# A two-layer hybrid attention block on one core: another order of loads, transposes and splits in the opening stage

## The chip, the cores and the metric

One core of a Trainium2 chip runs the whole program. The metric is device time in microseconds, the median of three runs; lower is better. Five engines work side by side: PE (TensorE: products and transposes), DVE (VectorE), ACT (ScalarE), POOL (GpSimd), and SP (SyncE), which here only issues DMAs. ACT and POOL issue DMAs too.

## What is computed

Two layers over 512 latent tokens `x` and 256 context tokens `ctx`, 1024 features each, all in fp32. Cut to what the change touches, which is the beginning of layer 0:

```python
c_act, c_ctx_act = silu(c), silu(c_ctx)                       # two vectors of 1024
sh1, sc1, g1, sh2, sc2, g2 = split(c_act @ w_mod[l] + b_mod[l], 6)      # the same from c_ctx_act for ctx
h_x = x * (1 + sc1) + sh1
h_c = ctx * (1 + csc1) + csh1
px, pc = h_x @ w_in[l], h_c @ w_in[l]                         # then three token mixers, merge, norm, FFN
```

`w_mod[l]` is 1024 by 6144. Of its twelve column blocks of 512, blocks 0 and 1 give the shift `sh1`, blocks 2 and 3 the scale `sc1`; only these four are needed before the first product with `h`. The other eight blocks of layer 0 are made later, between other work, and are not touched.

## The kernel before

Products are taken at fp32 precision by splitting: each operand is a `hi` part (rounded to fp32r by a cast) and a `lo` part (the rest, by a subtraction), and a product is three matmuls (`mm3`). So weights and activations are cast (usually on ACT) and subtracted (DVE, or POOL for some weights) before PE may use them. The activations `h` are kept feature-major: `h[0]` (hi) and `h[1]` (lo) are tiles of 128 by 8 by 768 fp32r.

All instructions are emitted inside `tc.manual_schedule()`: each engine runs its own instructions in the order in which the program emits them, and waits for what an instruction needs while later ones of that engine stand behind it. `Clock` (line 110) is a forecast kept by the program while it emits; `weave` (line 433), `At` and `Need` use it to decide how many steps of weight products are emitted between two steps of a latency-bound chain. `pump` (line 332) emits the loads of weights ahead into three `wr` buffers and one `wrf` buffer; `do_conv` (line 365) emits their splits.

The opening stage before the change:

- `setup` (line 501) makes silu of `c` and `c_ctx`; `setup_rows` (line 522) loads small parameters by POOL.
- `mod_block(0, blk, True)` (line 612) for blk 2, 0, 3, 1 makes four jobs each. A job loads 256 rows of `w_mod` (512 KB). Its products have 2 or 4 columns of `c` as the stationary side and 512 columns of weights moving. Of each block the first and last quarter are split (cast, subtract), the two in the middle go to PE as raw fp32. After the fourth quarter ACT copies the sums out of PSUM, and `post` (line 617) transposes them to columns.
- `build` (line 1789) emits the jobs of blocks 2 and 0 until the scale block 2 is done, then four loads of `x` on ACT's queue, then weaves `start0` (line 1807). That one issues three loads of the first 416 columns of `w_in` on ACT's queue, and then goes through `x` in two halves of the features: half 0 as soon as blocks 2 and 0 are there, half 1 after blocks 3 and 1. `mod_half` (line 780) transposes four blocks of a token tile to PSUM and applies scale and shift straight from PSUM (token tiles by turns on ACT and DVE); `mod_split` (line 797) of a tile is emitted after `mod_half` of the next one.
- The context tiles follow one by one (`mod_tile`, line 772), between the latent tiles' products with those 416 columns (`b1_tile`, line 821). The jobs of `win_jobs` (line 970), tiles of 128 other columns of `w_in`, fill PE in between; the first three are dq0, dk0 and dv0.
- `setup_cols` (line 543) and `setup_late` (line 561) are emitted after the last split of the latent tokens.

The line numbers of all calls in the profile are L106, the helper through which every instruction is emitted; so groups are told apart by their tiles: `wr`, `wh`, `wl` are a raw weight tile, its hi and lo part; `c` and `cact` the silu vectors; `ln` token tiles; `ac` and `h` scaled tokens and their split; `bc` the raw 416 columns and `s<-bc` their split; `b` and `S` are PSUM.

```python
self.split(hi, lo, src):   nc.scalar.copy(hi, src);  (lo_eng or nc.vector).tensor_tensor(lo, src, hi.bitcast(F32), ALU.subtract)
```

Of the kernel before, what the change touches and what calls it, by code (L numbers as in the profile page):

```python
# [97 lines left out]
class Port:  # L98
    """an engine's queue, each instruction noted by the clock before it is emitted"""
# [10 lines left out]
class Clock:  # L110
    """A coarse forecast, in us, of when each engine gets to what is put in its queue and when each tile is written.
    It only decides how many steps of the weight products are put between two steps of a latency-bound chain."""
# [63 lines left out]
    def transfer(self, t, c):  # L176
        """the first free stretch of the DMA rings from t on"""
# [44 lines left out]
class At:  # L222
    """go on when the products put in the queue reach this time"""
# [18 lines left out]
class Kern:  # L242
# [257 lines left out]
    # ---------------------------------------------------------------- setup  # L500
# [21 lines left out]
    def setup_rows(self):  # L522
        """loads of the small parameters, as rows"""
# [37 lines left out]
    def setup_late(self):  # L561
        nc, I, cp = self.nc, self.I, self.cp
        self.mask = cp.tile([P, NLEV, P], U8, name="mask")
        mv = self.mask[:].rearrange("p a b -> p (a b)")
        for a, b in ((0, 512), (512, NLEV * P)):
            mf = self.slab()
            nc.sync.dma_start(mf[:, :b - a], I["k_mask"][:, a:b])
            nc.vector.tensor_copy(mv[:, a:b], mf[:, :b - a])
        self.rm = cp.tile([P, TX], F32, name="rm")
        nc.sync.dma_start(self.rm[:], I["k_rope_m"])  # L570
        self.rk = cp.tile([P, 4, 2, 32], F32, name="rk")
        nc.sync.dma_start(self.rk[:].rearrange("p a b c -> p (a b c)"), I["k_rope_k"])
# [38 lines left out]
    # ---------------------------------------------------------------- adaLN modulation vectors  # L611
    def mod_block(self, l, blk, direct=False):
        nc, I = self.nc, self.I
        st = {}
        sec, half = blk // 2, blk % 2

        def post(mr):
# [19 lines left out]
            self.done.add(f"mod{l}_{blk}")  # L637

        def mk(u):
# [5 lines left out]
            def body(job):  # L645
# [5 lines left out]
                for k2 in range(2):  # L651
                    if job.conv is not None:
                        nc.tensor.matmul(ps[:2, :], self.cact[:].rearrange("p (a k) -> p k a", a=2)[:, 2 * u + k2, :],
                                         job.raw[:, k2 * 512:(k2 + 1) * 512], start=False, stop=False)
                        continue
# [3 lines left out]
                if job.conv is not None:  # L659
                    self.rawout[job.rk] -= 1  # L660
# [4 lines left out]
            j = Job(body, load, 1024)  # L665
            if direct:
                j.late = True
                if u in (1, 2):
                    j.conv, j.hold = (lambda j: None), True
            return j  # L670
# [86 lines left out]
    def affine(self, key, l, which, ln):  # L757
        """per-feature gain and offset of x -> x * (1 + sc) + sh, after the gain and offset of a layer norm if any"""
# [13 lines left out]
    def mod_tile(self, key, t, xo, h):  # L772
        """h[:, :, tile t] = transpose(xo) * A + B, split in two parts"""
# [35 lines left out]
    # ---------------------------------------------------------------- latent query/key front  # L809
# [185 lines left out]
    # ---------------------------------------------------------------- multi-head latent attention  # L995
# [136 lines left out]
    # ---------------------------------------------------------------- differential attention  # L1132
# [196 lines left out]
    # ---------------------------------------------------------------- bidirectional gated recurrence  # L1329
# [186 lines left out]
    # ---------------------------------------------------------------- gated merge  # L1516
# [132 lines left out]
    def ln_front(self, x1, r):  # L1649
        """x1 <- ALPHA * r + x1; the scale and offset of its normalization"""  # L1650
# [74 lines left out]
    # ---------------------------------------------------------------- FFN  # L1725
# [63 lines left out]
def build(ctx, tc, I, out):  # L1789
# [17 lines left out]
    def start0(xin):  # L1807
        K.b1w = []
        raws = [K.b1_load(0, u, K.nc.scalar.dma_start) for u in range(3)]
        prev = None  # L1810
        for g in range(2):
            for blk in ((2, 0), (3, 1))[g]:
                yield Need(f"mod0_{blk}")
            for i, t in enumerate(XT):
                hx = K.fp.tile([P, TX], F32, tag="ac", bufs=4, name=K.nm("ac"))
                yield from K.mod_half("in0", t, xin[t], g, hx[:], (K.nc.scalar, K.nc.vector)[i % 2])
                if prev:
                    yield from K.mod_split(K.h, *prev)
                prev = t, g, hx[:]
                if g == 1:  # L1820
                    yield At(K.ck.ready(raws[0]))
                    K.b1_conv(raws.pop(0))
                    if i == 0:
                        raws.append(K.b1_load(0, 3, K.nc.sync.dma_start))
            if g == 0:
                yield Need("mod0_3")
                for t in CT:
                    K.nc.scalar.dma_start(xin[t][:], res[t])
        yield from K.mod_split(K.h, *prev)
        K.done.add("hx0")  # L1830
        K.setup_cols()
# [15 lines left out]
    with tc.manual_schedule():  # L1847
# [3 lines left out]
        for blk in (2, 0, 3, 1):  # L1851
            for j in K.mod_block(0, blk, True):
# [141 lines left out]
```

## Time and profile before

| | |
|---|---|
| median of 3 runs | 3069.2 us (3064.12 to 3072.55) |
| span of the profiled execution | 3064.3 us |
| PE busy | 2825.8 us, 92% of the span |
| DVE, ACT, POOL busy | 53%, 37%, 32% |
| mean granted TensorE clock | 0.961 |
| moved by DMA | 359.14 MB, mean 117 GB/s |

The page gives the span of the profiled execution and no other time of it; the span is 4.9 us below the median of the runs and close to the fastest of them. "PEclk" is the granted share of TensorE's clock: 1.00 is 2.4 GHz and 0.50 is 1.2 GHz, and a value between is a stretch with both. A row of the timeline reads: start, duration, engine, line, operation, out<-in, shapes, count, and in brackets the idle time before it and what ended it. SPq, ACTq and POOLq are a queue's issues of DMAs; the duration of such a row is that of the issue, waits between merged issues included, not that of the transfer.

### The profile page before, as it was taken

Reading aid. Unit: us, or ns where it says so; the run is one execution under the profiler, and the core shown is the slowest. Engines: PE = TensorE matmul, PEld = TensorE weight load, DVE = VectorE, ACT = ScalarE, POOL = GpSimd, SP = SyncE. Lnnn points to the kernel's source line nnn. Section 1 sums busy time; section 2 is a strip of 40 time slices with the busy share of each in tenths; the row PEclk is TensorE's granted clock in tenths of the full one; section 3 lists DMA queues with packets and bytes.
Section 4 is the critical chain, followed back from the end, with each engine's and each line's share of the span. In section 5 each row is a group of like instructions: output and inputs, shape, how many; then the busy total and the mean of one; then the engine's idle time right before and its main releaser. Section 6 shows DMA issues by size and latency. Waiting matters only on the chain. (4 is left out here: it accounts for less than half of the span.)

```text
span 3064.3 us, 39087 instructions
## 1 busy us (share of the span) xinstructions
PE 2825.8 (92%) x14899; PEld 2346.2 (77%) x14899; DVE 1628.7 (53%) x2413; ACT 1137.7 (37%) x2177; POOL 974.2 (32%) x688
## 2 busy tenths in 40 slices
PE   6999989998799997999999898999998899799997
PEld 3888866677688885888888677887776777688875
DVE  4455566657762038555543665445656762632235
ACT  4544434443332124344332445444444332322222
POOL 1333433334444434243320223333324555300002
PEclk8999999999999998999999999999999999899998
DMA  6423243343333354354443354324223343433331
GB/s 211 129 80 97 91 136 96 100 141 103 101 111 110 103 169 151 117 152 143 119 137 96 110 167 122 89 83 131 79 73 127 104 132 123 146 107 96 103 131 69
DMA packets 345523, 359.14 MB, mean 117 GB/s; under 512 B 31114, under 2 KB 263044, under 8 KB 345336
## 3 DMA queue, kind: packets, MB, share of 16 engines
q1 hardware_dynamic: 343144, 351.84, 37.0%
q10 hardware_dynamic: 1680, 4.42, 0.4%
q8 instruction: 117, 1.92, 0.3%
q14 instruction: 70, 0.57, 0.1%
q0 software_dynamic: 512, 0.39, 0.1%
HBM read 298.10 MB, written 58.49 MB: 116 GB/s over the span
## 5 line engine op out<-in xcount | busy, mean ns | idle before, releaser
L106 PE MATMUL b<-h,wh 128*128 128x512 f32 (+1 forms) x5152 | 1385.0, 358 | 32.2 <-ACT h L106 14.2
L106 PEld LDWEIGHTS b<-h,wh 128*128 128x128 f32 x5152 | 911.5, 193 | 168.3 <-ACT h L106 15.1
L106 PE MATMUL b<-h,wl 128*128 128x512 f32 (+1 forms) x2576 | 909.5, 353 | 0.0
L106 DVE TENSOR_TENSOR wl<-wr,wh 128x1024 fp32r<-128x1024 f32 (+1 forms) x253 | 373.0, 1478 | 458.3 <-ACT wh L106 457.3
L106 PEld LDWEIGHTS b<-h,wl 128*128 128x128 f32 x2576 | 496.6, 193 | 66.4 <-DVE wl L106 0.3
L106 ACT CAST wh<-wr 128x1024 fp32r<-128x1024 f32 (+1 forms) x298 | 295.0, 993 | 415.2 <-PE b L106 331.2
L106 POOL TENSOR_TENSOR sm<-sm,mhalf 128x1 f32<-128x1 f32 (+3 forms) x80 | 56.7, 709 | 1035.7 <-DVE sm L106 1035.7
L106 POOL TENSOR_TENSOR wl<-wr,wh 128x1024 fp32r<-128x1024 f32 (+1 forms) x131 | 285.5, 2179 | 222.4 <-ACT wh L106 199.9
L106 ACT ACTIVATE s<-S,sm 128x768 f32<-128x768 f32 (+1 forms) x170 | 135.2, 796 | 377.7 <-DVE sm L106 325.2
L106 POOL TENSOR_TENSOR ln<-ln,wr 128x512 f32<-128x512 f32 x84 | 119.5, 1423 | 222.9 <-issue 161.6
L106 PE MATMUL S<-wh,ac 128*128 128x512 f32 x512 | 173.8, 404 | 16.4 <-DVE ac L106 11.2
L106 PE MATMUL S<-k,s 128*128 128x128 f32 (+2 forms) x704 | 150.8, 336 | 37.8 <-DVE k L106 33.8
L106 DVE TENSOR_TENSOR k<-b,k 128x512 fp32r<-128x512 f32 (+1 forms) x136 | 85.0, 627 | 175.0 <-ACT k L106 174.7
L106 PE MATMUL S<-k,k 96*128 96x512 f32 (+2 forms) x576 | 153.0, 366 | 22.8 <-DVE k L106 11.8
L106 PE MATMUL b<-k,wh 128*128 128x512 f32 (+1 forms) x576 | 161.5, 368 | 10.5 <-ACT k L106 6.9
L106 DVE TENSOR_REDUCE sm<-S 128x1 f32<-128x768 f32 (+1 forms) x160 | 131.5, 839 | 70.1 <-PE S L106 70.0
L106 PEld LDWEIGHTS S<-k,s 128*128 128x128 f32 (+1 forms) x704 | 107.4, 207 | 76.8 <-issue 51.2
L106 PEld LDWEIGHTS S<-k,k 96*128 96x128 f32 (+1 forms) x576 | 103.5, 196 | 63.4 <-issue 16.9
L106 PE MATMUL b<-ident,s 128*128 128x128 f32 (+3 forms) x687 | 111.8, 276 | 42.5 <-DVE s L106 19.3
L106 POOL TENSOR_SCALAR wh<-wr 128x1024 fp32r<-128x1024 f32 (+1 forms) x86 | 88.7, 1036 | 188.5 <-PE b L106 179.3
L106 POOL TENSOR_TENSOR s<-s,s 128x512 f32<-128x512 f32 (+2 forms) x88 | 112.4, 1288 | 90.2 <-DVE s L106 45.6
L106 DVE TENSOR_TENSOR k<-s,k 96x768 fp32r<-96x768 f32 (+7 forms) x92 | 108.8, 1209 | 52.3 <-ACT k L106 48.3
(184 smaller groups left out, 4128.5 us busy)
## 6 DMA issues: line engine op xcount, KB each, us to landing
wr<-in_w_ff_dram SPq DMA_DIRECT2D x154, 512.0 KB
wr<-in_w_mod_dram SPq DMA_DIRECT2D x96, 512.0 KB
d<-s SPq DMA_DIRECT2D x88, 384.0 KB
wr<-in_w_in_dram SPq DMA_DIRECT2D x64, 512.0 KB
s<-d SPq DMA_DIRECT2D x80, 384.0 KB
wr<-in_w_gate_dram SPq DMA_DIRECT2D x48, 512.0 KB
wr<-in_w_branch_dram SPq DMA_DIRECT2D x48, 256.0 KB
wr<-in_w_o_dram SPq DMA_DIRECT2D x24, 512.0 KB
```

What stands on the lines that cost most here:

```text
L106: return getattr(getattr(self.clock.nc, self.eng), op)(*a, **k)
```

## The change

The opening stage gets a function of its own, `front`. The sixteen quarter blocks of `w_mod` are loaded without waiting for buffers: twelve into the two tiles that will later hold `h`, three into `wr`, one into `wrf`. All loads of the stage are issued by SP in one sequence (eight of `w_mod`, four of `x`, eight of `w_mod`, two of `ctx`, three of `w_in`), but for four rows of `b_mod`, which ACT issues. `vectors` makes a block's products, `turn` transposes token tiles for one eighth of the features and copies them from PSUM to SBUF (eighths by turns on ACT and DVE), and `modulate` then scales and splits eighth by eighth, first all latent tokens and then all context tokens. `setup_cols` and the first part of the old `setup_late` (now `setup_bounds`) move into `front`. `start0` keeps the split of the 416 columns and the `b1_tile`s. `mod_block` loses its `direct` form.

```diff
+    def front(self, res):
+        nc, I, ck = self.nc, self.I, self.ck
+        blks = (2, 0, 3, 1)
+        big = [self.hp.tile([P, 6, D], F32, tag="h", name=self.nm("r")) for _ in range(2)]
+        raws = [big[i // 6][:, i % 6] for i in range(12)]
+        raws += [ck.ring("wr", 3, self.wp.tile([P, D], F32, tag="wr", bufs=3, name=self.nm("wr")))[:] for _ in range(3)]
+        raws.append(ck.ring("wrf", 1, self.fp.tile([P, D], F32, tag="wrf", bufs=1, name=self.nm("wr")))[:])
+        xin = {t: self.ln4() for t in XT + CT}
...
+        mrs = [self.slab() for _ in blks]
+        for i in range(8):
+            load(i)
+        for t in XT:
+            nc.sync.dma_start(xin[t][:], res[t])
+        for i in range(8, 16):
+            load(i)
+        for mr, blk in zip(mrs, blks):
+            nc.scalar.dma_start(mr[4:5, :512], I["b_mod"][0:1, blk * 512:(blk + 1) * 512])
+        for t in CT:
+            nc.sync.dma_start(xin[t][:], res[t])
+        b1 = [self.b1_load(0, u, nc.sync.dma_start) for u in range(3)]
+        xt = [self.slab() for _ in range(NK)]
+
+        def vectors(b):
+            ps = self.bank()
+            for u in range(4):
+                raw = raws[4 * b + u]
+                if u in (0, 3):
...
+                    self.split(hi[:], lo[:], raw)
...
+            nc.scalar.copy(mrs[b][:4, :512], ps[:4, :])
+
+        def turn(ks, tiles):
+            for k in ks:
+                ps = self.bank()
+                for i, t in enumerate(tiles):
+                    nc.tensor.transpose(ps[:, i * P:(i + 1) * P], xin[t][:, k * P:(k + 1) * P], self.ident[:])
+                o, n = tiles[0] * P, len(tiles) * P
+                (nc.vector.tensor_copy if k % 2 else nc.scalar.copy)(xt[k][:, o:o + n], ps[:, :n])
+
+        def modulate(ks, o, n, cx):
+            A, B = self.ab["in0"]
+            for k in ks:
+                s = xt[k][:, o:o + n]
+                nc.vector.tensor_scalar(s, s, A[:, k, cx:cx + 1], B[:, k, cx:cx + 1], ALU.mult, ALU.add)
+                self.split(self.h[0][:, k, o:o + n], self.h[1][:, k, o:o + n], s)
+
+        vectors(0)
+        vectors(1)
+        self.mod_post(0, 2)(mrs[0])
+        self.setup_cols()
+        turn(range(0, 4), XT)
+        self.mod_post(0, 0)(mrs[1])
+        self.setup_bounds()
+        vectors(2)
+        turn(range(4, 8), XT)
+        vectors(3)
+        self.mod_post(0, 3)(mrs[2])
+        turn(range(0, 4), CT)
+        self.mod_post(0, 1)(mrs[3])
+        turn(range(4, 8), CT)
+        self.h = self.new_h()
+        self.affine("in0", 0, 0, None)
+        modulate(range(8), XO, TX, 0)
+        self.done.add("hx0")
+        modulate(range(8), 0, TC, 1)
+        self.done.add("hc0")
+        return b1
...
-    def start0(xin):
+    def start0(raws):
         K.b1w = []
-        raws = [K.b1_load(0, u, K.nc.scalar.dma_start) for u in range(3)]
-        prev = None
-        for g in range(2):
...
-                K.setup_late()
+        for u in range(4):
+            yield At(K.ck.ready(raws[u]))
+            K.b1_conv(raws[u])
+            if u == 0:
+                raws.append(K.b1_load(0, 3, K.nc.sync.dma_start))
         K.setup_late()
         K.cr = [K.slab() for _ in range(4)]
-        yield from K.b1_tile(0, XT[0])
-        for i, t in enumerate(CT):
-            yield from K.mod_tile("in0", t, xin[t], K.h)
-            yield from K.b1_tile(0, XT[1 + i])
-        K.done.add("hc0")
-        for t in XT[3:] + CT:
+        for t in XT + CT:
             yield from K.b1_tile(0, t)
...
-        for blk in (2, 0, 3, 1):
-            for j in K.mod_block(0, blk, True):
-                K.add(j)
-        K.add(K.mod_flush()[0])
-        K.h = K.new_h()
+        raws = K.front(res)
         K.win = {}
         K.win_jobs(0, ndiff[:3])
-        K.affine("in0", 0, 0, None)
-        xin = {t: K.ln4() for t in order}
-        K.until("mod0_2")
-        for t in XT:
-            K.nc.scalar.dma_start(xin[t][:], res[t])
-        K.weave(start0(xin))
+        K.weave(start0(raws))
```

After the change `setup_late` holds only the loads of the masks and rope tables and the casts of the masks. Comments and docstrings are dropped throughout.

## Rows read from the trace of the kernel before

**Rows 1.** Busy time by stretch of the opening, granted clock, DMA share, GB/s.

```profile
32.00:41.00 9.00, 1.13 (x3) 0.30 (x4) 1.65 (x4) 1.80 (x2) 0.00 (x0) 0.53 1.04 405
41.00:60.00 19.00, 13.96 (x57) 7.47 (x54) 10.20 (x25) 12.36 (x27) 5.77 (x4) 0.77 0.57 161
60.00:70.00 10.00, 9.32 (x35) 8.57 (x36) 8.96 (x29) 6.39 (x15) 0.00 (x0) 0.67 0.39 129
70.00:100.00 30.00, 28.33 (x158) 26.40 (x158) 13.00 (x53) 18.14 (x60) 5.21 (x5) 1.00 0.00 1
100.00:122.60 22.60, 22.60 (x139) 20.31 (x138) 10.00 (x19) 9.31 (x20) 2.44 (x3) 1.00 0.64 146
```

(After stretch and length come PE, PEld, DVE, ACT and POOL, each busy us and number of instructions.)

**Rows 2.** Who waited for whom, 0 to 123 us: total, times, longest.

```profile
ACT wh L106 <- DMA wr<-in_w_mod_dram: 18.2, 6, 7.9
```

**Rows 3.** Timeline, ACT and its queue: first block, loads, evacuations.

```profile
4.74 0.21 ACT L106 CAST c<-cact 128x16 fp32r<-128x16 f32 x1 [0.24 <-DVE cact L106]
5.78 1.04 ACT L106 CAST wh<-wr 128x1024 fp32r<-128x1024 f32 x1 [0.83 <-DMA wr<-in_w_mod_dram]
...
27.74 1.34 ACTq L106 DMA_DIRECT2D ln<-in_x_dram  x3
28.65 0.57 ACT L106 COPY s<-b 4x512 f32<-4x512 f32 x1
...
31.81 6.19 ACTq L106 DMA_DIRECT2D bc<-in_w_in_dram  x3
38.10 1.04 ACT L106 CAST wh<-wr 128x1024 fp32r<-128x1024 f32 x1 [8.88 <-DMA ln<-in_x_dram]
...
40.24 1.05 ACT L106 CAST wh<-wr 128x1024 fp32r<-128x1024 f32 x1 [1.10 <-DMA wr<-in_w_mod_dram]
```

**Rows 4.** Timeline, PE: raw products, and the first and last products with `h`.

```profile
9.51 4.81 PE L106 MATMUL b<-wr,cact 128*2 128x512 f32 x8
...
25.28 3.60 PE L106 MATMUL b<-wr,cact 128*2 128x512 f32 x8
...
60.68 1.19 PE L106 MATMUL b<-h,wh 128*128 128x512 f32 x2 [2.89 <-DVE ac L106]
...
63.38 6.18 PE L106 MATMUL S<-s,h 128*128 128x416 f32 x24
69.39 0.60 PE L106 MATMUL b<-ident,ln 128*128 128x128 f32 x4
...
74.29 4.74 PE L106 MATMUL S<-s,h 128*128 128x416 f32 x24
...
122.57 0.63 PE L106 MATMUL b<-s,wh 128*128 128x512 f32 x2
```

**Rows 5.** Groups by shape over the whole span: busy us, mean ns, idle before.

```profile
L106 DVE TENSOR_TENSOR h<-ac,h 128x512 fp32r<-128x512 f32 x8 | 5.5, 682 | 0.1
...
L106 ACT CAST h<-ac 128x512 fp32r<-128x512 f32 x8 | 4.8, 616 | 1.1 <-DVE ac L106 1.1
...
L106 DVE TENSOR_SCALAR ln<-ln,sm,sm 128x1024 f32<-128x1024 f32 x16 | 17.0, 1061 | 0.0
...
L106 DVE TENSOR_SCALAR ln<-wr,cact 128x512 f32<-128x512 f32 x12 | 7.8, 651 | 0.0
```

**Rows 6.** Groups by shape, 0 to 60 us (first) and 0 to 123 us (last).

```profile
L106 DVE TENSOR_TENSOR wl<-wr,wh 128x1024 fp32r<-128x1024 f32 x8 | 9.8, 1224 | 26.4 <-ACT wh L106 26.4
...
L106 POOL TENSOR_TENSOR wl<-wr,wh 128x1024 fp32r<-128x1024 f32 x3 | 7.1, 2356 | 57.8 <-ACT wh L106 57.8
```

**Rows 7.** Timeline, DVE: bounds, from the first row to the last.

```profile
68.28 0.16 DVE L106 TENSOR_TENSOR lbm<-colv 128x8 f32<-128x8 f32 x1
...
73.16 0.14 DVE L106 TENSOR_SCALAR subg<-colv 128x1 f32<-128x1 f32 x1
```

**Rows 8.** Timeline: loads of SP's queue that waited for buffers, and the first one's cast.

```profile
8.11 7.63 SPq L106 DMA_DIRECT2D wr<-in_w_mod_dram  x5
...
11.75 1.04 ACT L106 CAST wh<-wr 128x1024 fp32r<-128x1024 f32 x1 [0.54 <-DMA wr<-in_w_mod_dram]
```

**Rows 9.** Timeline, DVE: the split of one raw tile of `w_in` columns.

```profile
61.04 1.09 DVE L106 TENSOR_TENSOR s<-bc,s 128x416 fp32r<-128x416 f32 x2
```

More of the change, by code (lines that the diff above doesn't have):

```diff
@@ L559, in setup_cols, with setup_bounds @@
         nc.scalar.copy(self.e2[:].rearrange("p a b -> p (a b)"), e2[:])
-    def setup_late(self):
+    def setup_bounds(self):
         nc, I, cp = self.nc, self.I, self.cp
[L563 to L572, printed above, removed]
         lg = self.colv[:, 96:112].rearrange("p (a d n) -> p a d n", a=2, d=2)
@@ L609, in setup_late, with mod_post @@
             self.subg.append(sg)
-    def mod_block(self, l, blk, direct=False):
-        nc, I = self.nc, self.I
-        st = {}
+    def setup_late(self):
+        nc, I, cp = self.nc, self.I, self.cp
+        self.mask = cp.tile([P, NLEV, P], U8, name="mask")
+        mv = self.mask[:].rearrange("p a b -> p (a b)")
+        for a, b in ((0, 512), (512, NLEV * P)):
+            mf = self.slab()
+            nc.sync.dma_start(mf[:, :b - a], I["k_mask"][:, a:b])
+            nc.vector.tensor_copy(mv[:, a:b], mf[:, :b - a])
+        self.rm = cp.tile([P, TX], F32, name="rm")
+        nc.sync.dma_start(self.rm[:], I["k_rope_m"])
+        self.rk = cp.tile([P, 4, 2, 32], F32, name="rk")
+        nc.sync.dma_start(self.rk[:].rearrange("p a b c -> p (a b c)"), I["k_rope_k"])
+    def mod_post(self, l, blk):
+        nc = self.nc
         sec, half = blk // 2, blk % 2
@@ L637, in post, with load @@
             self.done.add(f"mod{l}_{blk}")
+        return post
+    def front(self, res):
[6 more added lines that the diff above has]
+        xin = {t: self.ln4() for t in XT + CT}
+        def load(i):
+            blk, u = blks[i // 4], i % 4
+            w = I["w_mod"][0][u * 256:(u + 1) * 256, blk * 512:(blk + 1) * 512]
+            nc.sync.dma_start(raws[i].rearrange("p (k n) -> p k n", k=2), w.rearrange("(k p) n -> p k n", p=P))
+        mrs = [self.slab() for _ in blks]
[16 more added lines that the diff above has]
+                if u in (0, 3):
+                    hi = ck.ring("wh", 3, self.wp.tile([P, D], F32R, tag="wh", bufs=3, name=self.nm("wh")))
+                    lo = ck.ring("wl", 3, self.wp.tile([P, D], F32R, tag="wl", bufs=3, name=self.nm("wl")))
+                    self.split(hi[:], lo[:], raw)
+                for k2 in range(2):
+                    ks = slice(k2 * 512, (k2 + 1) * 512)
+                    if u in (0, 3):
+                        for wi, wt in enumerate((hi, lo)):
+                            nc.tensor.matmul(ps[:4, :], self.c4[:, 2 * u + k2, :], wt[:, ks],
+                                             start=(u == 0 and k2 == 0 and wi == 0), stop=(u == 3 and k2 == 1 and wi == 1))
+                    else:
+                        nc.tensor.matmul(ps[:2, :], self.cact[:].rearrange("p (a k) -> p k a", a=2)[:, 2 * u + k2, :],
+                                         raw[:, ks], start=False, stop=False)
+            nc.scalar.copy(mrs[b][:4, :512], ps[:4, :])
[33 more added lines that the diff above has]
+        return b1
@@ L639, in mk, with mod_block @@
+    def mod_block(self, l, blk):
+        nc, I = self.nc, self.I
+        st = {}
+        post = self.mod_post(l, blk)
         def mk(u):
@@ L651, in body @@
                 for k2 in range(2):
[L652 to L655, printed above, removed]
                     for wi, wt in enumerate((job.hi, job.lo)):
@@ L658, in body @@
                                          start=(u == 0 and k2 == 0 and wi == 0), stop=(u == 3 and k2 == 1 and wi == 1))
-                if job.conv is not None:
-                    self.rawout[job.rk] -= 1
                 yield 0.87
@@ L664, in body @@
                     self.modq.append((lambda: mr[:4], lambda: post(mr)))
[L665 to L670, printed above, removed]
+            return Job(body, load, 1024)
         return [mk(u) for u in range(4)]
@@ L1805, in entry @@
                 raws.append(K.b1_load(l, 3, nc.sync.dma_start))
-    def start0(xin):
+    def start0(raws):
         K.b1w = []
-        raws = [K.b1_load(0, u, K.nc.scalar.dma_start) for u in range(3)]
-        prev = None
-        for g in range(2):
[L1812 to L1827, printed above, removed]
-                    K.nc.scalar.dma_start(xin[t][:], res[t])
-        yield from K.mod_split(K.h, *prev)
-        K.done.add("hx0")
-        K.setup_cols()
+        for u in range(4):
[3 more added lines that the diff above has]
+                raws.append(K.b1_load(0, 3, K.nc.sync.dma_start))
         K.setup_late()
         K.cr = [K.slab() for _ in range(4)]
-        yield from K.b1_tile(0, XT[0])
-        for i, t in enumerate(CT):
-            yield from K.mod_tile("in0", t, xin[t], K.h)
-            yield from K.b1_tile(0, XT[1 + i])
-        K.done.add("hc0")
-        for t in XT[3:] + CT:
+        for t in XT + CT:
             yield from K.b1_tile(0, t)
```

1 line of the change is left out of this document (removed).

## The prediction

> **What bounds the kernel now.** I read first the busy time by stretch. From 70 us on PE has something to do almost all the time, 28.3 of 30 us and then 22.6 of 22.6; from 32 to 41 us it is nearly idle, and from 41 to 60 it is busy for 14.0 of 19 us, DVE for 10.2 and ACT for 12.4 [rows 1]. So the opening is a chain with gaps, and what follows is bound by PE. What the opening gains or loses is passed on, because PE has no gap to take it up.
>
> Then who waited for whom: in the opening ACT waits 18.2 us for loads of `w_mod` [rows 2], and 8.88 us in one other piece, of which the timeline shows what it is. ACT's queue issues four loads of `x` at about 0.45 us each, then needs 6.19 us for three loads of `w_in` columns, and ACT's next cast starts only behind them, at 38.10 [rows 3]. An issue can thus stand until earlier transfers have landed, and the engine stands with it. The last `w_mod` tile lands at 40.2 us [rows 3], in a stretch in which the DMA engines are full, at 405 GB/s [rows 1].
>
> Last the two ends of PE's work. The first product with `h` starts at 60.68. From 69.39 PE runs with hardly a gap to 122.57, where the next kind of job begins [rows 1, 4]. What remains from the first product with `h`: 122.57 - 69.39 = 53.2 us, less the context transposes (four groups like the one at 69.39, 2.4), plus the first `b1_tile` at the faster clock (4.74, its second instance), plus the six products ahead of it, at half of their 2.7 us since the clock there was partly the lower one (1.4): 57 us [rows 1, 4]. These are the same products after the change. So the question is when PE can start them.
>
> **The change part by part.**
>
> *Loads.* With nothing to wait for, SP keeps the DMA engines full. The first quarter lands at 5.78 [rows 3]; at 0.524 MB per 405 GB/s the others follow every 1.3 us, and with four tiles of `x` among them the sixteenth lands at 5.8 + 19 x 1.35 = 31.4, not 40.2. The three waits of ACT's queue are gone. In their place ACT issues four rows of `b_mod` ahead of its first cast, which moves from 5.78 to 4.95 + 4 x 0.45 = 6.75 [rows 3]. SP has only loads behind its waits. POOL's issues are the same. Raw tiles where `h` will be cost nothing: their last products end with the third block, long before `h` is written.
>
> *Vectors.* Loads would allow a block every 5 us. But ACT's order is: cast, cast, evacuate, and the evacuation waits for the block's last product; the next block's first cast stands behind it. One block is then a closed loop: cast 1.04, subtraction 1.22 [rows 3, 6], rest of the first products 0.7, raw products 3.44 (3.60 at the faster clock [rows 4]), last products 0.9, evacuation 0.57 [rows 3]: 7.9 us. The first evacuation starts at 6.75 + 7.45 = 14.2, the second at 22.2. Before the change the next block was split ahead, during those waits.
>
> *Columns, bounds, transposes.* These now stand in ACT's and DVE's order between blocks 2 and 3. DVE: the first block's columns 0.7, the small parameters 0.7, two copies of 512 from PSUM 1.3 (no such row; those of 512 elements take 0.65 and 0.68 [rows 5], a copy could be 0.53 by the 1024 row, and I take 0.65), again columns 0.5, then bounds, 4.9 us from first to last [rows 7]. In that stretch ACT waits several times for DVE, and the cast of the third block comes behind it, at about 30.4. It was hidden under products before; now nothing covers it. Third evacuation at 37.9, two copies of transposes on ACT (as the evacuation row, 0.57) and the fourth block to 47.5, its columns and the context's transposes to 50.8.
>
> *Clock.* Eight raw product rows took 4.81 us in the first block and 3.60 later [rows 4]; in the stretch with the longest PE gap the clock was 0.53 of full [rows 1]. PE now has gaps before the first and the third block. Bounds: 0 to 3.4 us for each of the four blocks; I take 1.3 for the first, by its own row, and 4.2 for the third with its other products. Modulation starts at 56.3.
>
> *Modulate.* DVE's order is scale, subtract, scale, subtract. The subtraction of an eighth needs ACT's cast of it, which needs its scaling; the next scaling stands behind. So the three add up: scaling 0.6, cast 0.62, subtraction 0.68 [rows 5], 1.9 with overlaps of starts; eight are 15.2 us, `hx0` at 71.5. For the scaling from SBUF of 512 the bounds are half of the 1024 row (0.53) and the other 512 row (0.65) [rows 5]. The Trainium skill ("VectorE: DVE Perf Modes", Mode 2x_2P) says that an fp32 tensor_scalar from SBUF runs at two results per cycle; by that the scaling would take an estimated 0.3 us, and the whole 3 us less. The row says 1061 ns for 1024, about one per cycle, and I go by the row. Context: half the width, 0.33 + 0.39 + 0.41, eight of 1.13, 9.0 us, ends at 80.5. Before the change a tile's split was emitted behind the next tile's scaling.
>
> *Behind it.* The split of the 416 columns stands behind the context on both engines: 1.1 us per raw tile on DVE [rows 9]. The first frees the buffer for SP's fourth load at +1.3. Behind that load in SP's order stand four small loads and then the weights of the first job, formerly loaded at 40 us: issues of 0.45 [rows 3], so at +3.5. From issue at 8.11 to the cast at 11.75 one load took 3.6 us [rows 8]; with 1.3 MB ahead of it I take 4.7, so +8.2. Cast 1.05, POOL's subtraction 2.36 [rows 6]: +11.6. `weave` emits six products of that job ahead of the first `b1_tile` (its forecast sees PE too early for `h`), so PE waits for this. Start 80.5 + 11.6 = 92.1; 57 us of products, 2 us for a slow clock at first: 151.1 against 122.57, 28.5 us later.
>
> **Sum.** +28 us: span 3064.3 to 3092. The runs' median lies 4.9 us above that span; on the median I predict 3097.
>
> **Rivals.**
>
> *The loads were the bound (faster).* For it: ACT's 18.2 + 8.9 us of waiting for DMAs [rows 2, 3]. If the vectors follow the loads, the last is ready some 5 us behind 31.4, and if scaling runs ahead of the subtractions, the first product starts at about 52: 52 + 59 - 122.6 = -11.6 us, 3058. It decides at the fourth evacuation: near 37 us, not 53. Against it: the order on ACT and DVE.
>
> *PE follows the splits (no change).* If weights of the first job are ready in time and PE takes eighth after eighth, it is dense from about 66: 66 + 59 - 122.6 = +2, 3072. Against it: the loads behind SP's wait.
>
> *ACT stands at the `b_mod` issues (slower still).* As before the cast at 38.10 [rows 3]. If these four wait for loads queued ahead of them, the first cast comes at about 26 instead of 6.75 and all behind it 20 us later: 3117. Against it: ACT gets to them at 5 us, when few loads have been issued.
>
> *Twelve quarters do not arrive early*, because issues wait for earlier ones to land. It changes nothing in the sum: the vectors, by their loop, need a block only every 8 us.
>
> **How the numbers follow.** Forecast 0.74, faster 0.07, no change 0.09, slower still 0.10. The forecast's own range: clock -5 to +8, scalings -1 to +2, weights -5 (if the `b1_tile` stands ahead of the job on PE) to +1, PE's remainder -3 to +4: 3083 to 3112. Extended to the slower case, 3083 to 3118 leaves out about 0.18. A measurement of this kernel can tell 0.3% (9 us) from no change; forecast and slower case lie beyond it: slower 0.84, same 0.09, faster 0.07.
>
> **What would show it.** Right: first `w_mod` cast near 6.8; evacuations 4x512 near 15, 23, 43 and 53; DVE's scalings of 128x512 from SBUF 1.9 us apart, each subtraction waiting for ACT; the last split of the context near 80; PE nearly idle from about 55 to 90; first product with `h` waiting for POOL's `wl`. Wrong: scalings back to back, products with `h` before 70 us, or the first job of the q up-projection before 135 us.

## The result and the profile after

The changed kernel is slower: 3095.44 us, median of 4 runs (3088.60 to 3099.25), against 3070.88 us of the kernel before in the same comparison (4 runs, 3064.12 to 3074.84); ratio 1.008, 95% interval 1.0066 to 1.0095. The profiled execution took 3095.5 us, its span is 3093.7 us, 29.4 more than before; mean clock 0.961 as before. The opening alone, up to the first job of the q up-projection, became 24.9 us longer: 147.47 against 122.57 [rows 4].

The page's first part; PE's busy time is about that of before (2825.8 us), since the products are the same:

```profile
span 3093.7 us, 39060 instructions
...
PE 2818.7 (91%) x14899; PEld 2337.8 (76%) x14899; DVE 1642.4 (53%) x2425; ACT 1131.6 (37%) x2156; POOL 977.0 (32%) x689
```

Busy time by stretch of the opening (columns as in [rows 1]):

```profile
0.00:32.00 32.00, 17.50 (x59) 5.20 (x59) 10.82 (x38) 9.81 (x17) 8.22 (x19) 0.98 0.96 345
32.00:56.00 24.00, 17.64 (x72) 6.47 (x72) 10.45 (x23) 8.26 (x14) 0.00 (x0) 0.89 0.24 94
56.00:88.60 32.60, 0.00 (x0) 0.00 (x0) 18.67 (x40) 12.20 (x24) 0.00 (x0) 0.53 0.27 76
```

The loads are now early: the DMA share is 0.96 up to 32 us and 0.24 from there to 56. But from 56.0 to 88.6 PE does nothing at all, while DVE is busy for 18.7 of 32.6 us and ACT for 12.2: neither is full, they wait for each other, and at the end of the stretch for a load of weights. Before, PE already had 9.3 of 10 us of work from 60 to 70 [rows 1]. The loss lies in that hole.

Who waited for whom, 0 to 150 us (answers to [rows 2]; total, times, longest):

```profile
ACT wh L106 <- DMA r<-in_w_mod_dram: 5.1, 2, 3.3
```

The timeline of ACT and its queue (answers to [rows 3]):

```profile
3.75 1.39 ACTq L106 DMA_DIRECT2D s<-in_b_mod_dram  x4
5.73 1.04 ACT L106 CAST wh<-r 128x1024 fp32r<-128x1024 f32 x1 [1.78 <-DMA r<-in_w_mod_dram]
...
16.12 0.57 ACT L106 COPY s<-b 4x512 f32<-4x512 f32 x1 [4.95 <-PE b L106]
...
24.40 0.58 ACT L106 COPY s<-b 4x512 f32<-4x512 f32 x1 [5.81 <-PE b L106]
...
32.07 1.98 ACT L106 CAST wh<-r 128x1024 fp32r<-128x1024 f32 x2
...
41.24 1.05 ACT L106 COPY s<-b 4x512 f32<-4x512 f32 x2 [7.19 <-PE b L106]
...
50.82 1.51 ACT L106 COPY s<-b 4x512 f32<-4x512 f32 x3 [5.80 <-PE b L106]
...
87.57 1.04 ACT L106 CAST wh<-wr 128x1024 fp32r<-128x1024 f32 x1 [3.87 <-DMA wr<-in_w_in_dram]
```

The `4x512` copies are the four evacuations. Each waits 5 to 7 us for PE, and the next block's cast stands behind it: the loads were there, and the pace did not follow them. The timeline of DVE, bounds first, then scaling and splitting:

```profile
27.95 0.16 DVE L106 TENSOR_TENSOR lbm<-colv 128x8 f32<-128x8 f32 x1
...
32.46 0.14 DVE L106 TENSOR_SCALAR subg<-colv 128x1 f32<-128x1 f32 x1
...
53.89 0.54 DVE L106 TENSOR_SCALAR s<-s,mc 128x512 f32<-128x512 f32 x1
55.11 0.69 DVE L106 TENSOR_TENSOR h<-s,h 128x512 fp32r<-128x512 f32 x1 [0.68 <-ACT h L106]
55.72 0.54 DVE L106 TENSOR_SCALAR s<-s,mc 128x512 f32<-128x512 f32 x1
...
77.97 0.42 DVE L106 TENSOR_TENSOR h<-s,h 128x256 fp32r<-128x256 f32 x1 [0.47 <-ACT h L106]
78.41 3.10 DVE L106 TENSOR_TENSOR s<-bc,s 128x416 fp32r<-128x416 f32 x6
```

A step of the latent tokens takes 55.72 - 53.89 = 1.83 us, of which DVE waits 0.68 for ACT's cast; the context ends at 78.39. SP's queue shows what then stood behind a buffer: the fourth load of 416 columns, then four small loads, then the first weights.

```profile
26.17 53.73 SPq L106 DMA_DIRECT2D bc<-in_w_in_dram  x4
79.94 0.94 SPq L106 DMA_DIRECT2D s<-in_k_mask_dram  x2
...
81.88 3.78 SPq L106 DMA_DIRECT2D wr<-in_w_in_dram  x3
```

And PE (answers to [rows 4]):

```profile
9.46 5.61 PE L106 MATMUL b<-r,cact 128*2 128x512 f32 x8
...
19.75 3.60 PE L106 MATMUL b<-r,cact 128*2 128x512 f32 x8
...
35.78 4.40 PE L106 MATMUL b<-r,cact 128*2 128x512 f32 x8
...
88.67 1.22 PE L106 MATMUL b<-h,wh 128*128 128x512 f32 x2 [35.16 <-ACT wh L106]
91.11 0.80 PE L106 MATMUL b<-h,wl 128*128 128x512 f32 x1 [1.22 <-POOL wl L106]
...
147.47 0.63 PE L106 MATMUL b<-s,wh 128*128 128x512 f32 x2
```

The first product with `h` waits for the cast of the weights, not for `h`.

### The profile page after: what moved, and what is told of

Same layout as the page of the kernel before. It is cut to its first block, busy times and chain, and to the rows that moved or that the text cites. A ratio compares the mean times of both kernels' runs of the same rounds, so it can differ in the third digit from the quotient of the medians.

```text
span 3093.7 us, 39060 instructions
## 1 busy us (share of the span) xinstructions
PE 2818.7 (91%) x14899; PEld 2337.8 (76%) x14899; DVE 1642.4 (53%) x2425; ACT 1131.6 (37%) x2156; POOL 977.0 (32%) x689
## 5 line engine op out<-in xcount | busy, mean ns | idle before, releaser
L106 ACT CAST wh<-wr 128x1024 fp32r<-128x1024 f32 (+1 forms) x291 | 287.4, 991 | 393.7 <-PE b L106 333.1
L106 PE MATMUL b<-k,wh 128*128 128x512 f32 (+1 forms) x576 | 162.3, 370 | 10.1 <-ACT k L106 7.1
```

The costliest lines, as they stand in the source:

```text
L106: return getattr(getattr(self.clock.nc, self.eng), op)(*a, **k)
```

## The experiments

Ten kernels. Downstream, executions of one kernel scatter by several us, so each is read by two places in its opening as well: the first product with `h` and the first product of the q up-projection ("q up"). Such a place is read from one profile, and the last section shows that the opening of one program moves by some 2 us between executions; a difference of that size is not read as a gain.

| kernel | first `h` | q up | median us | before, same comparison | ratio, 95% interval |
|---|---|---|---|---|---|
| before | 60.68 | 122.57 | | | |
| changed | 88.67 | 147.47 | 3095.44 | 3070.88 | 1.008 (1.0066 to 1.0095) |
| scale ahead | 80.99 | 140.02 | 3085.26 | 3066.46 | 1.0068 (1.0044 to 1.0091) |
| bounds late | 80.57 | 139.32 | 3087.48 | 3066.46 | 1.0075 (1.0051 to 1.0099) |
| weights early | 83.41 | 142.69 | 3088.21 | 3066.46 | 1.0067 (1.0048 to 1.0085) |
| split ahead | 82.82 | 141.08 | 3087.79 | 3066.46 | 1.0064 (1.0043 to 1.0086) |
| context later | 77.82 | 136.78 | 3082.49 | 3067.48 | 1.0047 (1.0032 to 1.0061) |
| the first four together | 61.23 | 120.03 | 3068.84 | 3072.11 | 0.9994 (0.9981 to 1.0006) |
| before, `w_in` columns by SP | 59.64 | 121.69 | 3067.69 | 3072.11 | 0.9991 (0.9977 to 1.0005) |
| reordered opening | 51.58 | 111.56 | 3056.98 | 3072.11 | 0.995 (0.9933 to 0.9967) |
| reordered, `w_mod` first | 42.79 | 103.96 | 3056.72 | 3072.11 | 0.9948 (0.993 to 0.9965) |
| the same, lo parts on DVE | 42.95 | 105.63 | 3059.22 | 3067.48 | 0.9967 (0.9954 to 0.998) |

At the end of the run most single edits are not resolved. Against the kernel before, in its own comparison, the changed kernel is 24.6 us slower; with one of the first four edits it is 18.8, 21.0, 21.8 and 21.3 us, and these intervals overlap that of the changed kernel. Context later (15.0) and the first four together (3.3 us faster) lie clear of it. So what a single edit is worth is read from the opening.

**Scale ahead.** Each eighth is scaled one step ahead of its cast and subtraction.

```diff
+            scale(ks[0])
             for k in ks:
-                s = xt[k][:, o:o + n]
-                nc.vector.tensor_scalar(s, s, A[:, k, cx:cx + 1], B[:, k, cx:cx + 1], ALU.mult, ALU.add)
-                self.split(self.h[0][:, k, o:o + n], self.h[1][:, k, o:o + n], s)
+                if k + 1 in ks:
+                    scale(k + 1)
+                self.split(self.h[0][:, k, o:o + n], self.h[1][:, k, o:o + n], xt[k][:, o:o + n])
```

> The changed kernel with one edit: each eighth is scaled one step ahead, so that DVE's order is scale, scale, subtract, scale, subtract. Theory A (order: scaling, cast and subtraction of an eighth add up only because the next scaling stands behind the subtraction): the scalings of 128x512 come 1.25 us apart instead of 1.83 (0.54 + 0.69 on DVE), those of 128x256 about 0.85 instead of 1.22; the context ends near 70.5 instead of 78.4, the first product with h near 81 instead of 88.7, the first product of the q up-projection near 139.5 instead of 147.5; the time is about 8 us below the changed kernel's 3095. Theory B (each step is as long as its engines need, or the weights loaded behind set the start): the period shrinks or not, but the first product with h stays within 1 us of 88.7.

Its DVE timeline:

```profile
56.29 1.00 DVE L106 TENSOR_SCALAR s<-s,mc 128x512 f32<-128x512 f32 x2
57.51 0.69 DVE L106 TENSOR_TENSOR h<-s,h 128x512 fp32r<-128x512 f32 x1 [0.23 <-ACT h L106]
...
58.58 0.69 DVE L106 TENSOR_TENSOR h<-s,h 128x512 fp32r<-128x512 f32 x1
...
66.47 0.41 DVE L106 TENSOR_SCALAR s<-s,mc 128x256 f32<-128x256 f32 x1
...
67.12 0.41 DVE L106 TENSOR_SCALAR s<-s,mc 128x256 f32<-128x256 f32 x1
```

Theory A: the wait is gone and a subtraction follows the other after 58.58 - 57.51 = 1.07 us, and the context's steps are 67.12 - 66.47 = 0.65 apart. It is more than expected (1.25 and 0.85), since starts overlap the ends of the instruction before. From the first scaling to the first product it is 24.7 us instead of 34.8. The q up-projection gains only 7.5, because modulation began at 56.29 instead of 53.89, for a reason told in the last section.

**Bounds late.** `setup_bounds` is called after the first `b1_tile` instead of between the second and the third block.

```diff
-        self.setup_bounds()
         vectors(2)
...
             yield from K.b1_tile(0, t)
+            if t == XT[0]:
+                K.setup_bounds()
```

> The changed kernel with one edit: the bounds and lambdas (setup_bounds) are emitted behind the first b1_tile instead of between the second and third block. Theory A (they are uncovered where the change put them): the third block's first cast moves from 32.1 to about 27.5, everything behind it by 4.6 us, the q up-projection from 147.5 to about 143; the time is 4 to 5 us lower. Theory B (the third block waits for its loads, or the copies of the transposes fill the gap): the third block's cast moves by under 1.5 us and the q up-projection stays within 1.5 us of 147.5.

Its ACT timeline, third block's casts and evacuation:

```profile
27.70 2.00 ACT L106 CAST wh<-r 128x1024 fp32r<-128x1024 f32 x2
35.52 1.05 ACT L106 COPY s<-b 4x512 f32<-4x512 f32 x2 [5.81 <-PE b L106]
```

Theory A: the cast comes 4.4 us earlier. The evacuation comes 5.7 earlier: cast to evacuation takes 7.8 us instead of 9.2. PE had no long gap ahead of this block (1.02 us instead of 5.90), the granted clock was 1.00 of full from 28 to 36 us, against 0.50 from 32 to 36 in the changed kernel, and the raw products took 3.60 instead of 4.40. So the bounds cost 4.4 us by themselves and 1.4 through the clock: modulation starts at 48.18 instead of 53.89. The q up-projection gains 8.2, and the other 2.4 us are a side effect: in this kernel SP issues the first weights (at 74.24) ahead of the four small loads (77.30), not behind them, and they are cast 6.8 us behind the end of the context instead of 9.2.

**Weights early.** The first three jobs' loads are issued behind the first three loads of 416 columns.

```diff
+        K.win = {}
+        K.win_jobs(0, ndiff[:3])
         raws = K.front(res)
...
+        self.pump(True)
         self.h = self.new_h()
```

> The changed kernel with one edit: SP issues the weights of dq0, dk0 and dv0 right behind the first three loads of the 416 columns, ahead of the fourth one and of the masks and rope tables. Theory A (PE's start waits for a load that stands behind a buffer wait in SP's order): ACT's cast of the first weights moves from 87.6 to about 83.7 (behind the splits of the 416 columns), POOL's first wl from 91.1 to about 87.2, the q up-projection from 147.5 to about 143.6. Theory B (the split of the 416 columns, ending at 84.4 on DVE, or the cast sets the start): the cast may move, the q up-projection stays within 1 us of 147.5.

Its ACT timeline, then POOL's:

```profile
79.68 2.73 ACT L106 CAST s<-bc 128x416 fp32r<-128x416 f32 x6
82.32 2.94 ACT L106 CAST wh<-wr 128x1024 fp32r<-128x1024 f32 x3
...
83.45 7.78 POOL L106 TENSOR_TENSOR wl<-wr,wh 128x1024 fp32r<-128x1024 f32 x3 [72.02 <-ACT wh L106]
```

Theory A: the cast follows the split with no wait for a load, 2.1 us behind the end of the context (80.23) instead of 9.2. The q up-projection gains only 4.8 us, since modulation began 1.8 us later here (55.72) than in the changed kernel, again without a cause in the edit; its second block has the slow raw products of the last section.

**Split ahead.** The next block's first split is emitted ahead of the present block's evacuation.

```diff
             ps = self.bank()
+            hl = [first.pop(b), wsplit(b, 3)]
+            if b < 3:
+                first[b + 1] = wsplit(b + 1, 0)
```

> The changed kernel with one edit: in the modulation vectors the first split of the next block is emitted ahead of the evacuation of the present one (for all four blocks), as the job list did before the change. Theory A (a block is a closed loop because its first cast stands behind the evacuation of the one before): the evacuations move from 16.1, 24.4, 41.2 and 50.8 to about 16, 21.5, 36 and 41.5; modulation starts near 45 instead of 53.9 and the q up-projection near 139 instead of 147.5. Theory B (loads set the pace): the casts then wait for w_mod, evacuations move by under 1 us each. Theory C (PE's slow clock sets the pace): the raw products stay at 4.8 us or more in all blocks and less than half of theory A's 8.5 us is gained.

Its ACT timeline:

```profile
25.12 1.04 ACT L106 CAST wh<-r 128x1024 fp32r<-128x1024 f32 x1 [5.44 <-DMA r<-in_w_mod_dram]
26.07 0.57 ACT L106 COPY s<-b 4x512 f32<-4x512 f32 x1
...
37.94 1.05 ACT L106 COPY s<-b 4x512 f32<-4x512 f32 x2 [1.27 <-PE b L106]
```

Theory A holds for the third and fourth block, though by less than expected (evacuations at 37.94 and 45.15, not 41.24 and 50.82; 36 and 41.5 were expected), and modulation starts at 48.21 instead of 53.89. In the second block the products end at 21.9 instead of 24.4, but theory B holds for its evacuation: the cast emitted ahead waits 5.44 us for a quarter that is loaded behind the four tiles of `x`, and the evacuation, whose products were done, stands behind it (26.07 instead of 24.40). With the closed loop opened, the loads are the next limit there.

**Context later.** The context is scaled and split behind the splits of the 416 columns, most of it behind the cast of the first weights.

```diff
-        modulate(range(8), 0, TC, 1)
-        self.done.add("hc0")
-        return b1
+        return b1, modulate
...
+            if u == 2:
+                modulate(range(2), 0, TC, 1)
+        K.do_conv(1)
+        modulate(range(2, 8), 0, TC, 1)
+        K.done.add("hc0")
         K.setup_late()
```

> The changed kernel with one edit: the context tokens are scaled and split behind the splits of the 416 columns (two eighths, to free the buffers, ahead of the fourth of these; the other six behind the cast of the first job's weights), so that most of them lie beside PE's products as before the change. Theory A (the 9 to 10 us of the context stand on the path to PE's first product): ACT's cast of the first weights comes at 76 to 78 instead of 87.6, the first product with h at 77 to 79 instead of 88.7, the q up-projection at 136 to 138 instead of 147.5; the time is 9 to 11 us lower. Theory B (the weights' landing, not the context, sets the start, or PE then waits for the context): the first product stays within 2 us of 88.7, or PE has a gap of several us behind the first b1_tiles.

The casts of its first weights on ACT:

```profile
76.72 1.04 ACT L106 CAST wh<-wr 128x1024 fp32r<-128x1024 f32 x1 [0.54 <-DMA wr<-in_w_in_dram]
```

Theory A in each number: first product with `h` at 77.82, q up-projection at 136.78, 10.7 us earlier. Not all of it is the context's. As in bounds late, SP issues the first weights (71.75) ahead of the four small loads (80.51), worth some 2.4 us there; and modulation started 1.7 us later than in the changed kernel (55.56), which works against the gain. The two nearly cancel, and the 9.8 us of the context are left.

**The first four together.**

> The changed kernel with the four edits together: scaling one step ahead, bounds behind the first b1_tile, first weights loaded early, next block split ahead. Theory A (four links of one chain, so their gains add, but for the gap between the second and third block that two of them fill): modulation starts near 42 to 45 instead of 53.9, the first product with h comes 17.8 us behind that, at 60 to 63, the q up-projection near 119 to 122, level with the kernel before (122.6) or up to 3 us ahead; the time is within 5 us of the kernel before. Theory B (the gains overlap, another limit such as the loads or PE's clock stands right behind): the first product with h after 70, the q up-projection after 128.

Theory A. Modulation starts at 44.16, the first product with `h` at 61.23, the q up-projection at 120.03. At that place the gains add up to 7.5 + 8.2 + 4.8 + 6.4 = 26.9 us apart from each other, 27.4 together, but in part by chance: scale ahead and weights early began modulation late, and bounds late has earlier weights in it. It is sounder to add them in the stretch that each edit works on. Up to the start of modulation bounds late and split ahead gain 5.7 us each and 9.7 together; two of the four fill the same gap, as expected. From there to the first product with `h` scale ahead gains 10.1 and weights early 7.1, together 17.7. The loss of the changed kernel is these uncovered stretches; without them, and with the context still uncovered, the early loads and the whole reordering are level with the kernel before (ratio 0.9994).

**The kernel before, with the 416 columns loaded by SP.**

```diff
-        raws = [K.b1_load(0, u, K.nc.scalar.dma_start) for u in range(3)]
+        raws = [K.b1_load(0, u, K.nc.sync.dma_start) for u in range(3)]
```

> The kernel before with one edit: SP instead of ACT issues the three loads of the 416 columns of w_in. Theory A (before the change, ACT standing at its issues held the opening; the new opening owes its gain on that side to SP issuing all): ACT's cast that stood at 38.10 comes near 32, and the q up-projection 3 to 5 us before 122.6. Theory B (the last w_mod quarters landed near 40 whatever ACT did, the loads were the bound there): the last w_mod cast stays within 1 us of 40.2 and the q up-projection within 1 us of 122.6.

Its casts of the last two split quarters on ACT (38.10 and 40.24 in [rows 3]):

```profile
33.97 1.04 ACT L106 CAST wh<-wr 128x1024 fp32r<-128x1024 f32 x1 [3.15 <-DMA bc<-in_w_in_dram]
43.92 1.04 ACT L106 CAST wh<-wr 128x1024 fp32r<-128x1024 f32 x1 [8.91 <-DMA wr<-in_w_mod_dram]
```

Neither theory in full. ACT's cast is 4.1 us earlier, but the last quarter, now issued behind the columns on SP, is cast 3.7 us later, and the q up-projection moves by 0.9. What ACT's long stand cost by itself is thus not shown: the edit took it away and held the last quarters of `w_mod` back at the same time.

**Reordered opening.** The four edits; quarters 0 to 3 in the weight buffers; splits of two raw tiles of columns in the fourth block and of two behind the latent tokens; the first weights cast amid the modulation; the context last.

```diff
+            else:
+                self.b1_conv(b1[0])
+                b1.append(self.b1_load(0, 3, nc.sync.dma_start))
+                self.b1_conv(b1[1])
...
+                if cx == 0 and k == 3:
+                    self.do_conv(1)
...
+        self.b1_conv(b1[2])
+        modulate(range(2), 0, TC, 1)
+        self.b1_conv(b1[3])
+        modulate(range(2, 8), 0, TC, 1)
```

> The four edits, and besides: the first quarters go to the weight buffers, so that the weights of the first jobs can be loaded without a wait; two raw tiles of the 416 columns are split during the fourth block, the other two behind the latent tokens; the first job's weights are split amid the modulation; the context tokens are scaled and split last, beside PE's products. Theory A (PE's start is set by the chain of splits alone): modulation starts near 43, the first product with h near 48, PE follows the splits and is dense from about 53, the q up-projection comes near 108 to 112; the time is 10 to 14 us below the kernel before. Theory B (what the opening gains is given back later, since PE is not the bound behind it): the q up-projection comes early, but the time gains less than half of that.

Theory A, a little late: modulation starts at 46.49 instead of near 43, the first product with `h` at 51.58, the q up-projection at 111.56, 11.0 us before the kernel before. The time is 15.1 us below it, so nothing was given back.

**The same, `w_mod` ahead of `x`.** The sixteen quarters are loaded first, the latent transposes come behind the fourth block, all splits of columns behind the latent tokens. Besides, the first weights are loaded ahead of the columns and cast behind the second eighth instead of the fourth.

```diff
-        for i in range(8):
+        for i in range(16):
             load(i)
         for t in XT:
             nc.sync.dma_start(xin[t][:], res[t])
-        for i in range(8, 16):
-            load(i)
```

> As the one before, and the sixteen loads of w_mod go ahead of the four of x, the transposes of the latent tokens move behind the fourth block, and all splits of the 416 columns behind the latent tokens. Theory A (in the one before, the third block waits for its first quarter, which lands at 25 behind the four loads of x): the third block's first cast comes near 20 instead of 25, modulation starts near 39 to 41, the q up-projection near 104 to 109. Theory B (x lands near 36 behind w_mod, and transposes and copies that were hidden now stand in the open): modulation starts at 43 or later, the q up-projection no earlier than in the one before.

Theory A: the third block's casts begin at 22.86 with no wait for a load, modulation at 40.08, the q up-projection at 103.96, 18.6 us before the kernel before. The time is no better than that of the last one (0.9948 against 0.995): the further 7.6 us are not seen at the end. Of the 30 us from the first product of the q up-projection on, PE is busy for 27.55, against 28.71 in the run before it, so about 1.2 us of them are lost there. Further on, one and the same cast on ACT starts at 133.54 in the trace of the run before and at 128.41 in this one, 5.1 us ahead, and one and the same subtraction on DVE at 776.64 and 777.07: by then the lead is gone. Which waits took it was not traced. Both beat the kernel before, and the changed one, beyond their intervals.

**Lo parts on DVE.** DVE instead of POOL subtracts for the first three weights.

```diff
-            K.win_jobs(0, ndiff[:3])
+            K.win_jobs(0, ndiff[:3], "vector")
```

> As the run with the loads of w_mod first, but DVE instead of POOL makes the lo parts of the first three weights (dq0, dk0, dv0). In that run a scaling of 128x512 on DVE took 2.58 us instead of 0.54 while POOL's subtraction ran, and one of 128x2 took 2.33 instead of 0.17. Theory A (DVE stands while POOL's subtraction of two SBUF operands runs): no scaling takes over 0.6 us and no 128x2 over 0.3; the lo part takes 1.2 us on DVE, so the latent tokens end about 0.9 us earlier, the first product with a lo part comes near 44 instead of 45.3; the q up-projection moves by 0 to -2 us. Theory B (the long rows have another cause, such as the cast on ACT or the landing loads): they stay long.

The timeline of POOL and DVE in the run before (with POOL subtracting), and below it DVE's in this one:

```profile
42.82 2.44 POOL L106 TENSOR_TENSOR wl<-wr,wh 128x1024 fp32r<-128x1024 f32 x1 [32.71 <-ACT wh L106]
...
42.97 2.58 DVE L106 TENSOR_SCALAR s<-s,mc 128x512 f32<-128x512 f32 x1
...
62.18 4.76 POOL L106 TENSOR_TENSOR wl<-wr,wh 128x1024 fp32r<-128x1024 f32 x2 [16.92 <-DMA rm<-in_k_rope_m_dram]
...
64.64 2.33 DVE L106 TENSOR_SCALAR sm<-sm 128x2 f32<-128x2 f32 x1
```

```profile
43.13 1.22 DVE L106 TENSOR_TENSOR wl<-wr,wh 128x1024 fp32r<-128x1024 f32 x1
44.26 0.54 DVE L106 TENSOR_SCALAR s<-s,mc 128x512 f32<-128x512 f32 x1
...
63.98 0.17 DVE L106 TENSOR_SCALAR sm<-sm 128x2 f32<-128x2 f32 x1
```

Theory A on the cause: the long rows are gone, and PE's first lo product starts at 44.40 instead of 45.31. But the q up-projection moved the wrong way, to 105.63, and the time did not improve. PE and POOL there say what is late next, a load of `w_uq`:

```profile
104.53 1.04 POOL L106 TENSOR_SCALAR wh<-wr 128x1024 fp32r<-128x1024 f32 x1 [12.54 <-DMA wr<-in_w_uq_dram]
...
105.63 1.22 PE L106 MATMUL b<-s,wh 128*128 128x512 f32 x2 [3.21 <-POOL wh L106]
```

SP issues these loads only from 98.64 on, behind two stores (`d<-s`) whose row in its queue lasts 27.39 us; in the reordered opening it issued them from 78.70 on.

## Why the prediction was right

The forecast case came: 3097 us were predicted and 3095.4 measured, and the mechanism is the one described: chains on ACT and DVE that nothing covers. Most of the views named as evidence show it. Two do not: the first cast did not come at 6.8, and the first product with `h` waited for ACT's cast of the weights; only the next one waited for POOL's `wl`. That the time came within 2 us is in part luck. The loss was 24.6 us, not 28, and the kernel before had a median of 3070.9 in this comparison, not 3069.2. By its own steps:

- *Loads early.* Right: ACT waits for `w_mod` twice, 5.1 us in all, instead of 18.2 [rows 2].
- *First cast at 6.75.* Wrong, at no cost: 5.73. The four issues of `b_mod` (3.75 to 5.14) ran while ACT waited for its first load anyway; each had been charged 0.45 us.
- *Closed loop of 7.9 us.* 8.28 from the first to the second evacuation. The split-ahead run shows the cause: there, with the same 3.60 us of raw products, the second block's products end 2.5 us earlier.
- *Columns and bounds.* The third block's first cast was forecast at 30.4 plus 1.3 of clock, and came at 32.07. Bounds late moved it by 4.4, of the 4.9 named.
- *Clock.* Mis-sized. The 4.2 us for the third block were 1.4, by the comparison of cast to evacuation with and without the gap (9.2 and 7.8). No row had given the 4.2; the raw products took 4.40 us there, 0.8 above the 3.60 of a granted clock of 1.00. In the first block they took 5.61, 2.0 above it, where 1.3 had been taken. The profile's clock column has 1.00 in that block, so it is not shown that this is the clock. All in all modulation started at 53.89 instead of 56.3.
- *Modulation.* Latent tokens 14.7 us (predicted 15.2), context 9.8 (9.0; a scaling of 256 takes 0.41, not 0.33). The step of 1.83 was forecast as 1.9, and scale ahead shows that the order of the two engines makes it.
- *Behind it.* 12.7 us from the end of the context to the first lo product (predicted 11.6): the weights were cast 9.2 us behind, not 8.2.
- *What remains.* 147.47 - 91.11 = 56.4, predicted 59: 57 us and 2 for a slow clock were too much by 2.6. Of these 1.2 are two of the six products in the 57, which ran ahead of the lo part, at 88.67; the rest was not told apart.

Together: -2.4 at the start of modulation, +0.3 in it, +1.1 behind it, -2.6 in the rest make the 3.6 between 28.5 and the 24.9 measured. The medians differ by 24.6; the two profiled spans by 29.4, so 4.5 us of that arise behind the opening in these two executions. They lie within the scatter of the runs and were not traced.

The rule weighed in the prediction was set aside on a row that was misread. The row gave 1061 ns as the mean of a scaling of 1024. The view of that tile in the kernel before has minimum, median and maximum instead (ns):

```profile
L106 DVE TENSOR_SCALAR ln<-ln,sm,sm x16: 800/804/2871, 1158.3 to 2677.1; 128x1024 f32<-128x1024 f32 x16
```

A scaling of 1024 takes 804; two of the sixteen, of 2.87 and 2.85 us, made the mean. The other bound, 0.65 for 512, is a mean of the same kind: its median is 0.48. With 0.54 for 512, a further 512 cost 0.26 us, 0.52 ns each, while the subtraction's rows (0.69 for 512, 0.42 for 256) give 1.05 ns each. The Trainium skill ("VectorE: DVE Perf Modes", Mode 2x_2P) has two results per cycle for such a scaling: in the rate it agrees with these rows. What the estimate of 0.3 us lacked is a fixed part of about 0.28 (0.54 - 0.26), so 0.54 and not 0.3, close to the 0.6 taken, by luck: the mean was too high, and the fixed part was left out. It changed the sum by less than 1 us.

The rivals: that the loads were the bound fell at the fourth evacuation (50.82, not 37). That PE follows the splits fell with the weights, which were cast only at 87.57. The `b_mod` issues held nothing up. Whether some quarters arrived late made no difference, as said: ACT waited for `w_mod` in the first block alone. Yet the reordered openings reached what that rival had hoped for, once the order on ACT and DVE was mended.

## What to carry to other kernels

Loading early moves the start only if the engines behind the loads are not chained by their own program order: write down, engine by engine, what stands behind each wait. Two engines that pass a tile back and forth need the next tile's first step emitted ahead of the present one's last; here that alone turned 1.83 us a step into 1.07. Setup work and the second group of tokens belong beside PE's products, not ahead of them; take a duration from the median of a row, not from its mean.

## What the runs showed of the hardware

**DVE stands while POOL subtracts.** With POOL's subtraction of two SBUF operands running (42.82 to 45.26), a scaling that takes 0.54 us took 2.58; on DVE instead of POOL the same lo part took 1.22 and the stall was gone. So the work given to POOL cost DVE 2.04 us there, more than the 1.22 of doing it. The Trainium skill ("SBUF — State Buffer", Terms, shared port pair) says that DVE and GpSimd arbitrate for one pair of ports, and that the loser is blocked for the other's whole instruction. These rows agree with it. So does the longest of the scalings that had spoilt the mean in the kernel before, by its timeline of POOL and DVE:

```profile
1756.48 5.17 POOL L106 TENSOR_TENSOR ln<-ln,bc 128x1024 f32<-128x1024 f32 x2 [2.49 <-PE b L106]
...
1756.54 2.87 DVE L106 TENSOR_SCALAR ln<-ln,sm,sm 128x1024 f32<-128x1024 f32 x1
```

It began 0.06 us behind the first of two such operations of POOL and took 2.87 us instead of 0.80.

**The same instructions, another clock.** Up to the second evacuation the changed kernel, scale ahead, bounds late, weights early and context later have the same instructions, but for the second block's raw products PE took 3.60 us in the changed kernel (at 19.75, above), 4.63 in bounds late and 5.29 in the other three. The row of scale ahead:

```profile
19.70 5.29 PE L106 MATMUL b<-r,cact 128*2 128x512 f32 x8
```

The changed kernel and scale ahead had both run the first product of that block in 0.40 us, with the same gaps before the next ones. Over the raw products the granted clock was 1.00 of full (2.4 GHz) in the changed kernel, and 0.68, a stretch with both levels, in scale ahead; 3.60 / 0.68 is 5.29, so the clock is the whole difference. By this alone the opening of one program moves by some 2 us between executions, so a gain of that size in an opening is not read from one profile.
